# A hybrid decoder step on one core: part-time constants become pages, the keys of the last block are split anew in each pass, and scheduling leads are set per half pass

## The chip, the core and the metric

The kernel runs on one core of one Trainium2 chip. The metric is the device time of one launch in microseconds (us), the median over runs. A profiled execution has a span (first to last instruction) and its own time, which is a little longer. The engines are PE (matrix), PEld (its weight loads), DVE (vector), ACT (scalar), POOL and SP, whose queue issues all DMAs of this kernel. Each engine executes its instructions in the order in which the program lists them.

## What is computed

One inference step of a two-branch layer, for a prompt of 2048 positions and for 8 sample sequences of one position, with width 1024 and float32 data. Cut to what matters:

```python
mod = silu(c) @ w_ada + b_ada                      # shift, scale, gate: 6 groups of 512 columns
h = rms_norm(x, norm_g) * (1 + scale) + shift
u = h @ w_in                                       # 43 column tiles of 128
o_a, wkv_new, shift_new = rwkv_mix(u_shifted, ...) # recurrence with a 64x64 state per head
q, k = rms_norm(q), rms_norm(k)
o_b = sliding_window_attention(q, k, v, window=128, bias, sinks)
merged = sigmoid(g_a) * ((o_a * silu(z_a)) @ w_o_a) + sigmoid(g_b) * ((o_b * silu(z_b)) @ w_o_b)
y = x + gate * (merged @ w_out)
```

The sample group uses the same weights, a stored 64x64 state per head (`state_wkv`), the last projected row and a cache of 128 keys and values.

## The kernel before, in words

**Passes and lines.** The 2048 positions are cut into four passes of 512 (pass 0 to 3). Pass 1 carries the 8 sample columns too, so its dense matmuls come in two pieces of 260 columns. A pass is 59 dense lines: 43 for the projections, in the order of ORDER (decay and rate, then r, k, v of four head pairs, k, v, four q, four z_b, four z_a, eight pairs of gates), 8 for the merge and 8 for the output. A line is 24 matmuls of 128x128 by 512, because each float32 product is made of three products of fp32r halves (`hi`, `lo`). In pass 0 the halves of the weights are made on ACT and DVE and written to DRAM; later passes load them (`weights`, L725).

**Recurrence.** `rwkv(g)` (L1548) does two head pairs: `prep_pair` (L969) makes the products inside chunks of 64; `inverses` (L1059) inverts the triangular matrices by a loop of 31 pairs of DVE instructions (a multiplication and a TENSOR_REDUCE on the tile `nl`), sends the result through DRAM (`d2`), transposes it on DVE (STREAM_TRANSPOSE) and finishes with two sets of 32x32 matmuls on PE; then comes the chain of 8 chunks, each three sets of 64-wide matmuls with copies and additions between them. This text calls the DVE loop with its round trip the solve; there is one per half pass, two per pass. `attention()` (L1553) does the k, v, q and z_b lines and four blocks of 128 queries (`attend`, L1237). With MIDDLE true (L1588) each pass does half 0 of the recurrence, then attention, then half 1.

**Sample work.** In pass 1 `sample_rwkv` (L1306) works through the stored state in four blocks: a load of `swkv` (L1366), some fifteen DVE operations on 128x512, six matmuls against `blocks`, and a store `out_wkvs`. `sample_attention` (L1399) does the cached attention.

**The order of the work.** The program is recorded first and then put in order by `schedule` (L286): an event-driven list scheduler with a cost for each operation, which picks on each engine the ready operation of the lowest priority number. That number is six times the line's index, less a lead. WLEAD (5000) is for weight loads, ELEAD (6000) for what empties a dense line's PSUM tile, and the table LEADS (L109) has one number per kind of step (prep, inv, chain, gn, att, sample and so on) and pass. A lead of thousands exceeds a whole pass (354), so in effect it ranks the kinds of work against each other on each engine. `places` (L321) holds an operation back until a tile is free: CAPS gives 75 pages `p` of 128x520 float32, 8 weight tiles `w`, one `nl`, 3 dense PSUM tiles `d` and 5 others `g`. The engines then run in the order that `schedule` wrote.

**Names that the change touches.** CAPS L108, LEADS L109, ADA L124, MIDDLE L127, `xst` L662, `sct` and `sc32` L688, `ada` L745, `us` L819, `kprev` L820 and L1583, `Lead` L829, `make_h` L860, `keys` L1216, `attend` L1237. ADA says in which order the first four groups of `w_ada` are taken; with False the group is split into fp32r halves (a cast and a subtraction on 128x512 and two matmuls per page), with True it is multiplied as float32 (nine rows, no split). `so` and `sob` are the sample results, `us` the sample columns of all 43 lines.

Of the kernel before, what the change touches and what calls it, by code (L numbers as in the profile page):

```python
# [87 lines left out]
def _constants():  # L88
# [18 lines left out]

CAPS = {"p": 75, "s": 11, "t": 14, "w": 8, "nl": 1, "d": 3, "g": 5}  # L108
LEADS = {  # L109
    "prep": (2490.0, 3436.9, 460.9, 3438.6),  # L110
    "inv": (2996.1, 5954.0, 5871.1, 5871.1),
    "chain": (3475.6, 3475.6, 3475.6, 3475.6),
    "gn": (2855.6, 4741.8, 4539.0, 2629.7),
    "wd": (2207.5, 3240.1, 1705.2, 3248.2),
    "norm": (4852.3, 820.0, 820.0, 820.0),
    "att": (4680.1, 4726.2, 4352.4, 4642.8),
    "sample": (1285.3, 1285.3, 1562.2, 1562.2),
    "bias": (2948.2, 5008.5, 5008.5, 5008.5),
    "h": (3088.9, 3088.9, 3088.9, 3109.5),
    "x": (209.4, 253.7, 253.7, 253.7),  # L120
}
WLEAD, ELEAD = 5000.0, 6000.0
HGATE = 6
ADA = ((2, False), (3, False), (0, True), (1, False))  # L124
EARLY, PLACE = 1, 3
KORDER = True
MIDDLE = True  # L127
FULL = dict(start=True, stop=True)
# [380 lines left out]
def hybrid_step_kernel(ctx: ExitStack, tc: tile.TileContext, A, O):  # L509
# [151 lines left out]
    ct = Sm([128, 8, 9])  # L661
    xst = K([128, 8, NB], "xst")  # L662
    dma(ct, A["ct"])
    dma(vec, A["vec"])
    dma(cst, A["cst"])
    dma(xst, A["xsT"])
    ident, mask = (cst[:, CST[n]:CST[n] + 128] for n in ["ident", "mask"])
# [19 lines left out]
    zero(eps[:, 2:3], KAPPA)  # L687
    sct = K([128, 8, 18], "sct", F32R)  # L688
    sc32 = K([128, 8, 9], "sc32")
    tht = Sm([128, 8, 9])  # L690
# [127 lines left out]
    zero(Sst)  # L818
    us = K([128, len(ORDER), NB], "us")  # L819
    kprev = [K([128, 128], f"kprev{i}", F32R) for i in range(4)]  # L820
    vprev = K([128, 128], "vprev")
# [4 lines left out]

    st = {"mm": [], "q": 0}

    class Lead:  # L829


        def __getitem__(self, name):
            return LEADS[name][min(st["q"], 3)]

# [25 lines left out]
    def make_h(q):  # L860
        sample = q == SQ
        w = W if sample else CH
        xs, acc = [], None
        for k in range(8):
            x = P([128, w])
            with after(*st.get("gate", ())):
                dma(x[:, 0:CH], A["xT"][k, :, q * CH:(q + 1) * CH])
                if sample:
                    copy(x[:, CH:W], xst[:, k, :], "dve/pool")
# [37 lines left out]
    def dense(key, epi):  # L907

        wt = early.pop(key, None) or weights("w_in", INDEX[key])
        for c0, n in st["segs"]:  # L910
            ps = pr.tile("d", [128, n])
            mm3(ps, wt, range(8), st["hk"], c0, n)
            m = min(c0 + n, CH) - c0
            with at(ELEAD):
                epi(ps[:, 0:m], c0, m)
                if c0 + n > CH:
                    copy(us[:, INDEX[key], :], ps[:, m:n])
        step_line()
# [296 lines left out]

    def keys(x):  # L1216

        out = [P([128, CH], F32R) for _ in range(4)]
# [17 lines left out]

    def attend(q, n, qn, kk, vt, bt, zb):  # L1237
        k0 = 128 if (q == 0 and n == 0) else 0
# [66 lines left out]

    def sample_rwkv(lw):  # L1306
        prev = Sm([128, 13, NB])
        dma(prev, A["sshift"])
# [46 lines left out]
        mul(bv, ps, v)  # L1355
        o = K([128, 4, NB], "so")
        idv = Sm([128, 64])
# [40 lines left out]

    def sample_attention():  # L1399
        iq, ik, iv = (INDEX[n, 0] for n in ("q", "kb", "vb"))  # L1400
        qk = Sm([128, 5, NB])
# [69 lines left out]
        add(ob, ob, pb)  # L1471
        o = K([128, 4, NB], "sob")
        obv = ob.rearrange("p (b h) -> p h b", h=8)
# [32 lines left out]
    def finish(q, j, ms, segs):  # L1506
# [5 lines left out]
        for c0, n in segs:  # L1512
# [3 lines left out]
            with at(ELEAD):  # L1516
                stt(xt[:, c0:c0 + m], ps[:, 0:m], modt[:, 16 + j, 0:1], xt[:, c0:c0 + m], ALU.mult, ALU.add)
                if c0 + n > CH:
                    t = Sm([128, NB])
                    mul(t, ps[:, m:n], modt[:, 16 + j, 1:9])  # L1520
                    add(t, t, xst[:, j, :])
                    dma(O["ysT"][:, j, :], t)
# [13 lines left out]
    for q in range(NQ):  # L1536
# [16 lines left out]
        def attention():  # L1553
            if q == 0:
                with at(LEAD["bias"]):
                    bias_table()
            x = plain(("kb", 0))
            with at(LEAD["norm"]):
                normed(x, vc("kg"))
                if q == NQ - 1:  # L1560
                    dma(O["kwp"], x[:, CH - 128:CH])
                kk = keys(x)
            x = plain(("vb", 0))
# [8 lines left out]
            here = line[0] * 6.0  # L1572
            zb = [gate_z(("zb", p)) for p in range(4)]
            pr.key = here - LEAD["att"]
            bt = [[P([128, 2, 256]) for _ in range(2)] for _ in range(2)]
# [146 lines left out]
```

## Time and profile before

| what | value |
|---|---|
| median of 3 runs | 1905.62 us (1904.24 to 1906.92) |
| profiled execution, own time | 1904.95 us |
| its span | 1903.1 us |
| mean granted PE clock | 0.984 |
| instructions in the span | 32620 |
| DMA | 343.20 MB, mean 180 GB/s |

The profiled execution's own time lies 0.67 us below the median of the runs, and its span 1.85 us below its own time. In the timeline a row gives start and length, engine, source line, operation, tiles and count; in square brackets stands how long the engine had been idle and what ended the wait. Almost all vector and scalar operations have line L538 and almost all dense matmuls L579, since helpers record them, so rows are told apart by their tiles and shapes. A float32 matmul counts as two instructions in the profile and as one in the program's order.

### The profile page before, as it was taken

Reading aid. Unit: us, or ns where it says so; the run is one execution under the profiler, and the core shown is the slowest. Engines: PE = TensorE matmul, PEld = TensorE weight load, DVE = VectorE, ACT = ScalarE, POOL = GpSimd, SP = SyncE. Lnnn points to the kernel's source line nnn. Section 1 sums busy time; section 2 is a strip of 40 time slices with the busy share of each in tenths; the row PEclk is TensorE's granted clock in tenths of the full one; section 3 lists DMA queues with packets and bytes.
Section 4 is the critical chain, followed back from the end, with each engine's and each line's share of the span. In section 5 each row is a group of like instructions: output and inputs, shape, how many; then the busy total and the mean of one; then the engine's idle time right before and its main releaser. Section 6 shows DMA issues by size and latency. Waiting matters only on the chain.

```text
span 1903.1 us, 32620 instructions
## 1 busy us (share of the span) xinstructions
PE 1807.5 (95%) x12544; PEld 1444.5 (76%) x12544; DVE 1302.0 (68%) x3138; ACT 798.5 (42%) x1605; POOL 93.9 (5%) x170
## 2 busy tenths in 40 slices
PE   6899999999999799899999999999999999999999
PEld 2667666677799778798998786677788787677787
DVE  8889979459377869792835795964563885894351
ACT  6667545353157355323504544521422562651300
POOL 0000210000000001010000100100000000100000
PEclk9999999999999899999999999999999999999999
DMA  9475537667845413453676453145467454236355
GB/s 335 175 265 213 172 110 273 222 231 283 320 158 175 145 68 102 161 189 118 211 245 201 145 183 119 67 157 186 150 228 249 158 177 141 72 125 194 113 192 187
DMA packets 162456, 343.20 MB, mean 180 GB/s; under 512 B 65485, under 2 KB 69246, under 8 KB 162300
## 3 DMA queue, kind: packets, MB, share of 16 engines
q1 hardware_dynamic: 162300, 341.11, 52.6%
q8 instruction: 99, 1.62, 0.3%
q14 instruction: 57, 0.47, 0.1%
HBM read 263.09 MB, written 77.96 MB: 179 GB/s over the span
## 4 chain that ended last, share of the span: by engine, by line
PE 48%; DVE 18%; ACT 4%; DMA 2%; issue 1%; SPq 1%; DVEq 0%; ACTq 0%
PE d L579 39%; DVE p L538 17%; PE g L597 5%; ACT p L538 3%; PE g L579 2%; PE g L604 2%; ACT L538 1%; DMA p<-in_xT 1%; DMA p<-d 1%; SPq L613 1%; DMA p<-in_swkv 0%; DVE t L538 0%; DMA w<-lo_w_in 0%; DVE s L538 0%; DMA d<-p 0%
## 5 line engine op out<-in xcount | busy, mean ns | idle before, releaser
L579 PE MATMUL d<-p,w 128*128 128x512 f32 (+1 forms) x7080 | 1457.4, 356 | 27.4 <-DVE w L538 15.8
L579 PEld LDWEIGHTS d<-p,w 128*128 128x128 f32 x7080 | 1140.5, 190 | 229.6 <-DVE w L538 26.8
L538 DVE TENSOR_TENSOR p<-p,p 128x512 fp32r<-128x512 f32 (+4 forms) x597 | 358.4, 624 | 33.8 <-ACT p L538 21.8
L597 PE MATMUL g<-p,p 128*64 128x64 f32 (+6 forms) x3952 | 229.1, 245 | 19.4 <-DVE p L538 16.6
L597 PEld LDWEIGHTS g<-p,p 128*64 128x64 f32 (+4 forms) x3952 | 174.7, 144 | 85.8 <-DVE p L538 27.0
L538 ACT COPY p<-g 64x128 f32<-64x128 f32 (+4 forms) x339 | 124.0, 377 | 138.9 <-PE g L597 89.9
L538 ACT CAST p<-p 128x512 fp32r<-128x512 f32 (+2 forms) x201 | 121.5, 621 | 135.6 <-DVE p L538 132.6
L538 ACT ACT_TABLE_LOAD x109 | 139.8, 1283 | 22.9 <-PE g L579 20.4
L538 ACT ACTIVATE p<-d 128x512 f32<-128x512 f32 (+1 forms) x120 | 61.4, 512 | 209.0 <-PE d L579 208.6
L538 DVE TENSOR_TENSOR p<-g,s 64x128 f32<-64x128 f32 (+1 forms) x124 | 40.5, 326 | 141.4 <-PE g L597 136.8
L538 DVE TENSOR_TENSOR p<-p,nl 128x2 f32<-128x2 f32 (+30 forms) x248 | 126.9, 512 | 8.9 <-DMA p<-in_idl 3.7
L538 ACT ACTIVATE p<-d,vec 128x511 f32<-128x511 f32 (+1 forms) x65 | 38.9, 603 | 214.8 <-PE d L579 178.5
L538 DVE SCALAR_TENSOR_TENSOR p<-d,modt,p 128x512 f32<-128x512 f32 (+2 forms) x40 | 25.7, 644 | 124.7 <-PE d L579 115.1
L538 ACT ACTIVATE p<-p 128x512 f32<-128x512 f32 (+2 forms) x161 | 98.1, 633 | 17.4 <-DVE p L538 9.7
L538 DVE TENSOR_TENSOR w<-w,w 128x1024 fp32r<-128x1024 f32 x58 | 70.8, 1221 | 41.2 <-PE d L579 23.5
L579 PE MATMUL g<-p,blocks 128*128 128x512 f32 x202 | 81.8, 436 | 17.5 <-ACT p L538 11.0
L538 ACT CAST w<-w 128x1024 fp32r<-128x1024 f32 x59 | 61.9, 1050 | 83.7 <-PE d L579 51.6
L538 DVE SCALAR_TENSOR_TENSOR p<-p,d 128x512 f32<-128x512 f32 (+1 forms) x120 | 69.3, 579 | 36.9 <-PE d L579 35.8
L538 DVE TENSOR_TENSOR p<-g,cst 64x256 f32<-64x256 f32 (+1 forms) x192 | 88.6, 507 | 3.9 <-PE g L597 3.1
L538 DVE TENSOR_REDUCE p<-p 128x1 f32<-128x2 f32 (+30 forms) x248 | 86.7, 349 | 5.3
L604 PE MATMUL g<-cst,p 128*128 128x128 f32 (+1 forms) x457 | 74.3, 285 | 8.3 <-DVE p L538 7.5
L604 PEld LDWEIGHTS g<-cst,p 128*128 128x128 f32 (+1 forms) x457 | 54.8, 144 | 31.2 <-DVE p L538 12.2
(159 smaller groups left out, 1060.2 us busy)
## 6 DMA issues: line engine op xcount, KB each, us to landing
w<-hi_w_in SPq DMA_DIRECT2D x129, 512.0 KB, 3.6
w<-lo_w_in SPq DMA_DIRECT2D x129, 512.0 KB, 4.5
w<-in_w_in SPq DMA_DIRECT2D x43, 512.0 KB, 4.8
hi_w_in<-w SPq DMA_DIRECT2D x43, 512.0 KB, 3.5
lo_w_in<-w SPq DMA_DIRECT2D x43, 512.0 KB, 4.2
p<-in_xT SPq DMA_DIRECT2D x64, 256.0 KB, 5.8
p<-in_w_ada SPq DMA_DIRECT2D x48, 256.0 KB, 5.5
w<-hi_w_o SPq DMA_DIRECT2D x24, 512.0 KB, 3.6
```

Of the source, the lines that this page charges most:

```text
L538: lambda e: getattr(ENG[e], engs[e])(res(out), *(res(x) for x in a), **{n_: res(v) for n_, v in k.items()}),
L579: pr.rec({"pe": mm_cost(out, lhsT, rhs)}, lambda e: nc.tensor.matmul(res(out), res(lhsT), res(rhs), **k), [out], [lhsT, rhs], table=(part( ...
L597: nc.tensor.matmul(res(out), res(lhsT), res(rhs), **k)
L604: pr.rec({"pe": 2 * _free_size(in_) / 2400.0 + 0.003}, lambda e: nc.tensor.transpose(res(out), res(in_), res(idn)), [out], [in_, idn], tab ...
L613: lambda e: nc.sync.dma_start(out=res(out), in_=res(in_)),
```

## The change

1. `xst`, `us`, `so` and `sob` share one page, which is allocated in pass 1 and filled there (the load of `xst` moves from the start of the program into `make_h`). `sct` and `sc32` become pages that live through pass 0. CAPS gives 77 pages in place of 75.
2. The keys of the last block of a pass are kept once, in float32 (`klast`), and the four fp32r forms are made anew at the start of the next pass by `keys`; before, four fp32r copies were kept (`kprev`).
3. ADA takes the groups 0, 2, 1, 3, two of them split and two whole; before 2, 3, 0, 1 with one whole.
4. LEADS has eight numbers per kind, one for each half of a pass; `attend` sets its priority for each block.
5. MIDDLE is replaced by STAGES: pass 1 does both halves of the recurrence and then attention; the other passes keep attention in the middle.

```diff
-CAPS = {"p": 75, "s": 11, "t": 14, "w": 8, "nl": 1, "d": 3, "g": 5}
+CAPS = {"p": 77, "s": 11, "t": 14, "w": 8, "nl": 1, "d": 3, "g": 5}
 LEADS = {
...
-    "sample": (1285.3, 1285.3, 1562.2, 1562.2),
+    "sample": (5619.9, 5482.5, 7295.5, 7295.5, 7295.5, 7295.5, 7295.5, 5619.9),
...
-ADA = ((2, False), (3, False), (0, True), (1, False))
+ADA = ((0, False), (2, True), (1, False), (3, True))
-MIDDLE = True
+STAGES = ('0A1', '01A', '0A1', '0A1')
...
-    xst = K([128, 8, NB], "xst")
-    dma(xst, A["xsT"])
...
-    sct = K([128, 8, 18], "sct", F32R)
-    sc32 = K([128, 8, 9], "sc32")
+    sct = P([128, 8, 18], F32R)
+    sc32 = P([128, 8, 9])
...
-    us = K([128, len(ORDER), NB], "us")
-    kprev = [K([128, 128], f"kprev{i}", F32R) for i in range(4)]
+    klast = K([128, 128], "klast")
...
-            return LEADS[name][min(st["q"], 3)]
+            return LEADS[name][2 * min(st["q"], 3) + st["half"]]
...
+        if sample:
+            n = len(ORDER)
+            page = P([128, n + 16, NB])
+            st.update({"us": page[:, 0:n], "xst": page[:, n:n + 8], "so": page[:, n + 8:n + 12], "sob": page[:, n + 12:n + 16]})
+            with after(*st.get("gate", ())):
+                dma(st["xst"], A["xsT"])
...
-                kk = keys(x)
+                kprev = []
+                if q > 0:
+                    before = P([128, 4, 128], F32R)
+                    kprev = keys(klast, [before[:, i, :] for i in range(4)])
+                kk = keys(x, [P([128, CH], F32R) for _ in range(4)])
+                copy(klast, x[:, CH - 128:CH], "dve/pool")
...
             for n in range(4):
-                attend(q, n, qn, kk, vt, bt, zb)
-            for i in range(4):
-                copy(kprev[i], kk[i][:, CH - 128:CH], "dve/pool")
+                st["half"] = n // 2
+                pr.key = here * 6.0 - LEAD["att"]
+                attend(q, n, qn, kk, kprev, vt, bt, zb)
...
-        if MIDDLE:
-            rwkv(0)
-            yb = attention()
-            rwkv(1)
-        else:
-            rwkv(0)
-            rwkv(1)
-            yb = attention()
+        for stage in STAGES[min(q, 3)]:
+            if stage == "A":
+                yb = attention()
+            else:
+                rwkv(int(stage))
```

**How the order moves.** On PE, pass 0 keeps its order after the `w_ada` groups. The counts below are of dense matmuls in the order of PE, for before and after: from the start of pass 1 to its first 32x32 matmul 840 and 965; from there to the first 32x32 matmul of the second half 966 and 403; from the first 32x32 matmul to the last product of attention 238 and 814 in pass 1, 141 and 168 in pass 2, 134 and 148 in pass 3. On DVE, 450 rows stand between the transposes of the first half's solve and those of the second in pass 1 before; after, 164 stand there, and 428 from the first half's transposes to the end of attention. In DVE's whole order there are 20 TENSOR_TENSOR fewer (POOL has 20 more) and 26 COPY fewer (ACT has 26 more).

PE in pass 1, at the end of the first half's solve, before (`p_1203` is the transposed solve, rows of 128x260 are dense lines, 128x256 are attention's products of q and k):

```order
L579 MATMUL d_220<-p_925_4603,w_1170_6181 128x260
L579 MATMUL d_220<-p_924_4595,w_1171_6189 128x260
L597 MATMUL g_221<-p_1203_6477,p_1053_5408 32x32 x16
L597 MATMUL g_221<-p_1203_6477,p_1097_5691 32x32 x16
L597 MATMUL g_222<-p_1107_5757,p_1134_5932 128x256
L597 MATMUL g_222<-p_1114_5805,p_1134_5932 128x256
```

The same place after (`p_1228` is the transposed solve):

```order
L579 MATMUL d_211<-p_860_4304,w_1196_6467 128x260
L579 MATMUL d_211<-p_864_4321,w_1196_6467 128x260
L597 MATMUL g_214<-p_1228_6701,p_1042_5374 32x32 x16
L597 MATMUL g_214<-p_1228_6701,p_1080_5666 32x32 x16
L579 MATMUL d_211<-p_860_4304,w_1198_6476 128x260
L579 MATMUL d_211<-p_872_4356,w_1196_6467 128x260
```

Attention is no longer there: eleven dense matmuls stand between the two sets of 32x32 matmuls in place of eight products of attention.

SP's queue in pass 1 around the second load of the stored state, before (`nl` is the solve's tile of the second half, `w` are weight tiles):

```order
L613 DMA d_1_95<-p_1432_7820 32x8x32 x2
L613 DMA out_wkvs<-p_1400_7634 128x512
L613 DMA nl_1467_8028<-d_1_95 64x1024 x2
L613 DMA w_1474_8059<-hi_w_in_158 128x1024
L613 DMA w_1476_8064<-lo_w_in_159 128x1024
L613 DMA p_1477_8069<-in_swkv 128x512
```

The same queue after, around the second and third loads:

```order
L613 DMA out_wkvs<-p_1317_7362 128x512
L613 DMA w_1438_8197<-hi_w_in_159 128x1024
L613 DMA w_1444_8220<-lo_w_in_160 128x1024
L613 DMA p_1446_8232<-in_swkv 128x512
L613 DMA w_1468_8361<-hi_w_in_161 128x1024
L613 DMA w_1469_8368<-lo_w_in_162 128x1024
L613 DMA out_wkvs<-p_1446_8232 128x512
L613 DMA p_1479_8424<-in_swkv 128x512
```

The loads of `nl` no longer stand ahead of the second load; they come before the first one. Now the third load stands directly behind the store of the second block, and the fourth behind that of the third.

More of the change, by code (lines that the diff above doesn't have):

```diff
@@ L106, in _constants @@
     return c, one, np.eye(128, dtype=np.float32)[::-1], idl
-CAPS = {"p": 75, "s": 11, "t": 14, "w": 8, "nl": 1, "d": 3, "g": 5}
+CAPS = {"p": 77, "s": 11, "t": 14, "w": 8, "nl": 1, "d": 3, "g": 5}
 LEADS = {
[L110 to L116, printed above, removed]
-    "sample": (1285.3, 1285.3, 1562.2, 1562.2),
-    "bias": (2948.2, 5008.5, 5008.5, 5008.5),
-    "h": (3088.9, 3088.9, 3088.9, 3109.5),
-    "x": (209.4, 253.7, 253.7, 253.7),
+    "prep": (2430.9, 2430.9, 3436.9, 3436.9, 452.9, 452.9, 3438.6, 3438.6),
+    "inv": (2996.1, 2996.1, 5811.5, 5811.5, 5933.5, 5933.5, 5960.9, 5960.9),
+    "chain": (3475.6, 3475.6, 3475.6, 3463.5, 7297.1, 7297.1, 3457.1, 3475.6),
+    "gn": (2855.6, 3546.9, 4741.8, 195.1, 4539.0, 4539.0, 2629.7, 2629.7),
+    "wd": (2207.5, 2207.5, 3240.1, 3240.1, 1757.7, 1757.7, 3248.2, 3248.2),
+    "norm": (4852.3, 4852.3, 820.0, 820.0, 796.4, 820.0, 820.0, 820.0),
+    "att": (4680.1, 4566.4, 4726.2, 4726.2, 4352.4, 4352.4, 4642.8, 4642.8),
+    "sample": (5619.9, 5482.5, 7295.5, 7295.5, 7295.5, 7295.5, 7295.5, 5619.9),
+    "bias": (2948.2, 2948.2, 5008.5, 5008.5, 5008.5, 3968.7, 5008.5, 5008.5),
+    "h": (3088.9, 3088.9, 3088.9, 3088.9, 3084.9, 3084.9, 2964.3, 3084.9),
+    "x": (390.0, 390.0, 390.0, 394.3, 390.0, 390.0, 0, 390.0),
 }
@@ L825, in hybrid_step_kernel @@
            for i in range(2)]
-    st = {"mm": [], "q": 0}
+    st = {"mm": [], "q": 0, "half": 0}
     class Lead:
         def __getitem__(self, name):
-            return LEADS[name][min(st["q"], 3)]
+            return LEADS[name][2 * min(st["q"], 3) + st["half"]]
     LEAD = Lead()
@@ L868, in make_h @@
                 if sample:
-                    copy(x[:, CH:W], xst[:, k, :], "dve/pool")
+                    copy(x[:, CH:W], st["xst"][:, k, :], "dve/pool")
             sq = P([128, w])
@@ L916, in dense @@
                 if c0 + n > CH:
-                    copy(us[:, INDEX[key], :], ps[:, m:n])
+                    copy(st["us"][:, INDEX[key], :], ps[:, m:n])
         step_line()
@@ L1214, in queries, with keys @@
         return out
-    def keys(x):
-        out = [P([128, CH], F32R) for _ in range(4)]
+    def keys(x, out):
         for e, h in enumerate((lo, hi)):
@@ L1235, in values, with attend @@
         return vt
-    def attend(q, n, qn, kk, vt, bt, zb):
+    def attend(q, n, qn, kk, kprev, vt, bt, zb):
         k0 = 128 if (q == 0 and n == 0) else 0
@@ L1306, in sample_rwkv @@
     def sample_rwkv(lw):
+        us = st["us"]
         prev = Sm([128, 13, NB])
@@ L1355, in sample_rwkv @@
         mul(bv, ps, v)
-        o = K([128, 4, NB], "so")
+        o = st["so"]
         idv = Sm([128, 64])
@@ L1399, in sample_attention @@
     def sample_attention():
+        us = st["us"]
         iq, ik, iv = (INDEX[n, 0] for n in ("q", "kb", "vb"))
@@ L1471, in sample_attention @@
         add(ob, ob, pb)
-        o = K([128, 4, NB], "sob")
+        o = st["sob"]
         obv = ob.rearrange("p (b h) -> p h b", h=8)
@@ L1520, in finish @@
                     mul(t, ps[:, m:n], modt[:, 16 + j, 1:9])
-                    add(t, t, xst[:, j, :])
+                    add(t, t, st["xst"][:, j, :])
                     dma(O["ysT"][:, j, :], t)
@@ L1548, in rwkv @@
         def rwkv(g):
+            st["half"] = g
             for p in (2 * g, 2 * g + 1):
@@ L1553, in attention @@
         def attention():
+            st["half"] = 0
             if q == 0:
@@ L1571, in attention @@
                     qn.append(queries(x))
-            here = line[0] * 6.0
+            here = line[0]
             zb = [gate_z(("zb", p)) for p in range(4)]
-            pr.key = here - LEAD["att"]
+            pr.key = here * 6.0 - LEAD["att"]
             bt = [[P([128, 2, 256]) for _ in range(2)] for _ in range(2)]
@@ L1580, in attention @@
             for n in range(4):
-                attend(q, n, qn, kk, vt, bt, zb)
-            for i in range(4):
-                copy(kprev[i], kk[i][:, CH - 128:CH], "dve/pool")
+                st["half"] = n // 2
+                pr.key = here * 6.0 - LEAD["att"]
+                attend(q, n, qn, kk, kprev, vt, bt, zb)
             copy(vprev, vt[:, 3], "dve/pool")
@@ L1586, in attention @@
             return zb
-        if MIDDLE:
-            rwkv(0)
-            yb = attention()
-            rwkv(1)
-        else:
-            rwkv(0)
-            rwkv(1)
-            yb = attention()
+        for stage in STAGES[min(q, 3)]:
[3 more added lines that the diff above has]
+                rwkv(int(stage))
+        st["half"] = 0
         if sample:
@@ L1599, in hybrid_step_kernel @@
             sob = sample_attention()
-            silu2(sob, us[:, INDEX["zb", 0]:INDEX["zb", 0] + 4, :])
+            silu2(sob, st["us"][:, INDEX["zb", 0]:INDEX["zb", 0] + 4, :])
             for p in range(4):
@@ L1607, in hybrid_step_kernel @@
             if sample:
-                silu2(so, us[:, INDEX["za", 0]:INDEX["za", 0] + 4, :])
+                silu2(so, st["us"][:, INDEX["za", 0]:INDEX["za", 0] + 4, :])
             ya = []
```

## The prediction

> **What bounds the kernel now.** I read the page first, then the busy time by stages, the waits of PE, and the timeline around the two longest of them. The page's first part:
>
> ```profile
> PE 1807.5 (95%) x12544; PEld 1444.5 (76%) x12544; DVE 1302.0 (68%) x3138; ACT 798.5 (42%) x1605; POOL 93.9 (5%) x170
> ```
>
> PE is busy 95% of the span, and the change takes almost no matmul away, so only the 95.6 us in which PE is idle (1903.1 - 1807.5) and the time that it works slowly can be won. The table of stretches shows where the idle time lies: first length, then busy time of PE, PEld, DVE, ACT and POOL, then the granted clock.
>
> ```profile
> 24.00:41.30 17.30, 16.43 (x61) 5.41 (x62) 15.87 (x31) 8.57 (x15) 0.60 (x4) 1.00 1.05 392
> 524.00:658.50 134.50, 123.09 (x1004) 119.09 (x1002) 104.59 (x262) 74.63 (x138) 6.67 (x9) 0.98 0.51 166
> 658.50:745.00 86.50, 81.89 (x884) 67.81 (x885) 64.03 (x219) 50.22 (x146) 9.17 (x18) 0.94 0.19 64
> 745.00:865.50 120.50, 110.97 (x864) 106.94 (x862) 100.39 (x253) 35.48 (x79) 8.67 (x10) 0.96 0.55 178
> 865.50:1012.00 146.50, 146.35 (x1487) 140.43 (x1487) 68.47 (x156) 37.06 (x78) 3.25 (x11) 1.00 0.57 195
> 1012.00:1153.00 141.00, 136.88 (x675) 109.87 (x673) 108.82 (x275) 72.53 (x125) 8.76 (x13) 1.00 0.53 172
> 1153.00:1250.00 97.00, 90.50 (x793) 62.54 (x794) 77.31 (x219) 52.77 (x138) 9.89 (x11) 0.95 0.24 78
> 1597.00:1695.00 98.00, 90.66 (x812) 63.53 (x813) 77.14 (x222) 53.08 (x139) 9.67 (x13) 0.95 0.24 79
> ```
>
> Pass 1 runs from 524 to 1012: PE is idle for 11.4 + 4.6 + 9.5 + 0.2 = 25.7 us in it, nearly all of that before 865, while DVE is nearly full. After 865 PE lacks nothing and DVE is less than half busy. Pass 2's part with chain and attention (1153 to 1250) loses 6.5 us, pass 3's 7.3 us. Where PE idles in pass 1, its waits say:
>
> ```profile
> PE g L597 <- DVE p L538: 12.3, 7, 9.5
> PE g L579 <- ACT p L538: 7.3, 4, 6.7
> ```
>
> Two single waits, 9.5 and 6.7 us, are most of it. A slow clock follows them; these stretches of the same table have a granted clock of 0.50:
>
> ```profile
> 652.00:669.00 17.00, 9.43 (x150) 8.68 (x151) 7.96 (x29) 4.46 (x12) 0.30 (x1) 0.50 0.20 32
> 802.00:808.80 6.80, 4.86 (x18) 4.49 (x19) 4.65 (x11) 1.61 (x3) 0.00 (x0) 0.50 0.31 123
> 1157.00:1163.80 6.80, 6.80 (x78) 4.97 (x80) 2.71 (x8) 1.46 (x5) 0.00 (x0) 0.50 0.01 3
> ```
>
> Work at half clock loses half its time: 9.43 / 2 = 4.7 us and 4.86 / 2 = 2.4 us in pass 1, and up to 6.8 / 2 = 3.4 us in pass 2.
>
> **The first wait: the solve.** PE, DVE and SP around 658 us (the number in brackets is the idle time before the row):
>
> ```profile
> 637.55 11.45 PE L579 MATMUL d<-p,w 128*128 128x260 f32 x94
> 658.50 0.31 PE L597 MATMUL g<-p,p 32*32 32x32 f32 x2 [9.50 <-DVE p L538]
> 651.74 0.69 DVE L538 TENSOR_REDUCE p<-p 128x16 f32<-128x512 f32 x1
> 652.46 1.26 SPq L613 DMA_DIRECT2D d<-p  x2
> 658.01 0.90 DVE L538 STREAM_TRANSPOSE p<-p 32x256 f32<-32x256 f32 x2 [4.93 <-DMA p<-d]
> ```
>
> The loop ends on DVE at 652.4, the round trip through DRAM takes until 658, and PE had run out of its 94 dense matmuls at 649. These take 11.45 / 94 = 0.12 us each. From pass start to this place the order of PE has 840 dense matmuls before and 965 after: 125 x 0.12 = 15 us more cover. But two more pairs of preparation stand on DVE ahead of the solve now. In the row 524.00:658.50 DVE has 134.5 - 104.6 = 29.9 us free. A pair's preparation takes a share of the 100.39 us that DVE works from 745 to 865, where two pairs, sample work and the second loop (some 25 us) lie; I take 15 us for a pair at most, 30 us for two. So DVE needs up to 30 us more, fits it into 29.9 + 15 us, and the wait shrinks. I take 8 of the 9.5 us as won; the bounds are 9.5 and nothing.
>
> **The second wait: a load of the stored state.** SP, DVE and PE:
>
> ```profile
> 793.41 1.13 SPq L613 DMA_DIRECT2D nl<-d  x2
> 795.69 0.42 SPq L613 DMA_DIRECT2D p<-in_swkv  x1
> 802.54 0.69 DVE L538 TENSOR_TENSOR p<-p,s 128x512 f32<-128x512 f32 x1 [2.69 <-DMA p<-in_swkv]
> 803.94 0.80 PE L579 MATMUL g<-p,blocks 128*128 128x512 f32 x1 [6.72 <-ACT p L538]
> 812.19 0.38 SPq L613 DMA_DIRECT2D p<-in_swkv  x1
> 820.14 0.69 DVE L538 TENSOR_TENSOR p<-p,s 128x512 f32<-128x512 f32 x1
> ```
>
> The load is queued behind two loads of `nl`, which wait for the solve's data, and it is used 802.54 - 795.69 = 6.9 us after its issue; PE stands 6.72 us. The third load has 820.14 - 812.19 = 8.0 us until its use and costs nothing. After, `nl` is loaded long before, so this wait goes: -6.7 us. But the third and fourth loads stand right behind the stores of the block before, which wait for DVE, and DVE's order has about 15 rows between the store's last addition and the next use. At 100.39 / 253 = 0.40 us a row that is 6 us against the 6.9 us of this load: a wait of about 1 us on DVE at one or two loads. Sum -5 us; from -6.7 (no new wait) to +7 (two new waits as long as the old, 2 x 6.7 - 6.7).
>
> **The half clock in pass 1.** If both waits go, 4.7 + 2.4 = 7.1 us of slow work go with them. A short slow stretch stays, as in pass 2 (1157.00:1163.80), where no wait is longer than 2 us. I take -6 us, from -7.1 to 0. The Trainium skill ("TensorE: Matmul & The Clock Gate", the part on the clock gate and its table of two states) says that the array drops to half its clock after an idle window of about 3.4 us and recovers after about as long of sustained work. The rows at 652 and 802 agree with that; the row at 1157 does not, since PE is busy through all of it. By that rule alone pass 2 and 3 could win nothing from their half clock, and the sum below would be 2 us less.
>
> **What takes their place in pass 1.** The work of 658 to 865 is not removed, only arranged anew: chain 0 now runs beside the second solve, chain 1 beside the sample work and the start of attention. From the first transposes to the end of attention the order of DVE has 428 rows after; 450 stood between the two solves' transposes before, and these took 64.03 + 100.39 = 164.4 us of DVE. So DVE has 428 x 164.4 / 450 = 156 us there. PE has 814 dense matmuls in that stretch, 98 us, against 966 before, 116 us; before, PE was busy 81.89 + 110.97 = 192.9 us there. Less 18 us of dense work, and with one chain more and two preparations fewer, that is some 175 us. PE stays the longer of the two, but closely, and every chain step, sample block and attention block waits on a DVE that is 156 / 175 = 89% full. Before, the same stretch lost 4.6 + 9.5 - 6.7 = 7.4 us to waits that are not the load. I add 4 us: +4, from 0 to +15 (twice the 7.4 again).
>
> **Passes 2 and 3.** Their waits behind the solve are short:
>
> ```profile
> 1147.82 4.79 PE L579 MATMUL d<-p,w 128*128 128x512 f32 x20
> 1156.89 0.75 PE L579 MATMUL d<-p,w 128*128 128x512 f32 x1 [1.82 <-DVE p L538]
> 1159.42 4.21 PE L579 MATMUL d<-p,w 128*128 128x512 f32 x9
> ```
>
> A dense matmul takes 4.79 / 20 = 0.24 us, at half clock 4.21 / 9 = 0.47. From the solve to the end of attention the order has 27 dense matmuls more in pass 2 (141 to 168) and 14 more in pass 3 (134 to 148): 6.5 and 3.4 us of cover, against 6.5 and 7.3 us of idle time. Six dense matmuls now stand between the two sets of 32x32 ones where one stood, which covers the 1.82 us wait nearly (5 x 0.24 = 1.2 us). Not all cover falls where a wait is; I take half, 3 and 2 us, together -5, from -11 (all 9.9 us and 1 us of clock) to +3, since chain and attention are mixed anew.
>
> **The start.** Before the first dense matmul two groups of `w_ada` are split in place of three:
>
> ```profile
> 14.03 0.61 PE L579 MATMUL d<-p,sct 128*18 128x512 f32 x1 [14.03 <-ACT p L538]
> 32.13 3.60 PE L579 MATMUL d<-p,sc 128*9 128x512 f32 x8
> 34.93 3.26 DVE L538 TENSOR_TENSOR p<-p,p 128x512 fp32r<-128x512 f32 x5
> 33.66 1.66 ACT L538 CAST p<-p 128x512 fp32r<-128x512 f32 x3
> 38.79 2.71 PE L579 MATMUL d<-p,sct 128*18 128x512 f32 x11
> 41.34 0.62 PE L579 MATMUL d<-p,w 128*128 128x512 f32 x2
> ```
>
> A group fewer takes 8 x 3.26 / 5 = 5.2 us from DVE and 8 x 1.66 / 3 = 4.4 us from ACT. PE gives up 16 matmuls of 2.71 / 11 = 0.25 us, 3.9 us, and gets a whole group, 2 x 3.60 = 7.2 us: 3.3 us more. PE is busy 16.43 of 17.30 us from 24 to 41.3 (it starts at 14.03, as before), so the 3.3 us count; DVE is busy 15.87 of 17.30 us, so its 5.2 us count where PE waits for it afterwards. The two nearly cancel: 0, from -4 to +3.
>
> **The rest.** The page for the sample columns, the constants as pages, and two more pages add no instruction on PE. The new split of the last keys is 8 small operations per pass on half the partitions, in three passes, less 4 copies in each:
>
> ```profile
> L538 ACT COPY p<-g 64x128 f32<-64x128 f32 (+4 forms) x339 | 124.0, 377 | 138.9 <-PE g L597 89.9
> ```
>
> At 377 ns that is 24 x 0.377 = 9 us, shared by ACT (42% busy) and DVE, ahead of attention, whose first products have dense lines before them. That cover hides it: 0; without it 3 us per pass.
>
> **The sum.** Pass 1: -8 - 5 - 6 + 4 = -15. Passes 2 and 3: -5. Start and rest: 0. From the profiled execution's 1904.95 us (span 1903.1 and 1.85 around it; 0.67 us below the median) that gives 1885 us.
>
> **Rivals.** *All idle time of pass 1 goes.* 25.7 us of waits and 7.1 us of clock, with 10 us in passes 2 and 3: 1904.95 - 42.8 = 1862 us. For it speaks that the second half of pass 1 has room (68.47 of 146.5 us on DVE); against it, that DVE stays 89% full in the crowded stretch.
>
> *The waits move and nothing is won.* The solve ends as late as before because its loop shares DVE with four preparations, and DVE has 20 other rows between the end of the loop and the transposes where 2 stood (8 us at 0.40). Then only the load's wait and its clock go (6.7 + 2.4), and the crowded stretch gives back 7.4: about 1903 us. The same comes out if the tables and pages change little of what is waited for.
>
> *Slower: the sample's chain starves PE.* The sample lead (1285 to 7295) now lies above what empties the dense tiles (6000), and each of four blocks runs load, DVE, PE, DVE, store, load, with the next load behind the store. If DVE's 15 rows between store and use take less than the load's 6.9 us, in-order DVE stands still, epilogues behind it keep the three dense PSUM tiles, and PE stops: three loads at 6.7 us and their clock at 2.4 are 27 us. Less the old load (9.1) and the solve (8): 1904.95 + 10 = 1915 us. It decides at about 6 us of DVE work per block; I counted 6, so it is close, but DVE also has attention to do meanwhile.
>
> **How the numbers follow.** Forecast 0.59, all idle time 0.12, nothing won 0.14, slower 0.15. The forecast's own terms end at 1872 and 1899 when two of them are at a bound. The range, 1864 to 1909 us, takes in the case without gain and half of the best one, and part of the slower one. About 0.2%, 3.8 us, is what a measurement of this kernel can tell from no change. Faster by more: 0.59 + 0.12 + a third of the case without gain, 0.76; within it 0.10; slower by more 0.14.
>
> **What would show it.** Right: in pass 1 no wait of PE over 3 us before the first 32x32 matmul nor at a `blocks` matmul of the sample, pass 1 about 15 us shorter than 488 us, no half clock of 17 us; passes 2 and 3 each 2 to 3 us shorter; first dense matmul at 41 to 44 us. Wrong: a wait of DVE on `in_swkv` or on the round trip of `d` with PE idle behind it, idle time of PE in pass 1 above 20 us, or a pass 0 that changes by more than 4 us.

## The result and the profile after

The changed kernel takes 1883.12 us (median of 4 runs, 1882.18 to 1886.82); the kernel before, run beside it, 1904.93 us (1902.86 to 1906.92). The ratio is 0.9889 (95% interval 0.9872 to 0.9907), about 21 us less; all ratios below, too, are to the kernel before, run beside the kernel in question. Of all runs in this text one was slow, a run of the changed kernel with 75 pages that took 2895 us at a granted clock of 0.57, and it is left out of the figures. The profiled execution has a span of 1880.9 us. The forecast was 1885 us, and the whole came out so. Its parts did not, and the rest of this text is about them.

The page's first part of the changed kernel:

```profile
PE 1797.0 (96%) x12544; PEld 1438.7 (76%) x12544; DVE 1284.6 (68%) x3098; ACT 803.7 (43%) x1629; POOL 110.5 (6%) x184
```

PE's idle time is 1880.9 - 1797.0 = 83.9 us where it was 95.6, so idle time explains 12 us of the 22; the other 10 are matmuls that ran at a faster clock or stalled less. The same stretches by pass show where. The borders are the first dense matmuls of the passes; first the kernel before, then the changed one, with length, busy time of PE, PEld, DVE, ACT and POOL, granted clock, DMA share and GB/s:

```profile
41.34:524.24 482.90, 454.62 (x2771) 335.14 (x2770) 368.76 (x808) 245.57 (x445) 25.05 (x38) 0.99 0.64 227
524.24:1011.71 487.47, 461.77 (x4232) 433.82 (x4231) 337.39 (x886) 197.38 (x441) 27.76 (x48) 0.97 0.48 160
1011.71:1456.63 444.92, 433.56 (x2731) 333.55 (x2729) 287.20 (x698) 172.46 (x352) 23.83 (x38) 0.99 0.50 164
1456.63:1903.10 446.47, 431.72 (x2727) 332.91 (x2725) 275.42 (x674) 158.03 (x328) 15.53 (x28) 0.99 0.46 153
```

```profile
42.59:523.14 480.55, 453.21 (x2763) 334.37 (x2763) 367.04 (x805) 244.53 (x446) 24.22 (x37) 0.99 0.64 227
523.14:1009.69 486.55, 462.83 (x4232) 433.48 (x4230) 332.20 (x871) 198.85 (x452) 38.77 (x57) 0.97 0.48 160
1009.69:1444.27 434.58, 425.91 (x2730) 330.05 (x2729) 283.42 (x692) 177.02 (x363) 24.05 (x40) 1.00 0.51 168
1444.27:1880.90 436.63, 426.41 (x2727) 330.73 (x2725) 269.91 (x661) 160.33 (x334) 21.52 (x32) 0.99 0.47 157
```

Pass 1, from which 15 us were forecast, gives 0.9. Passes 2 and 3, from which 5 were forecast, give 10.3 and 9.8. The start costs 1.2 us, and pass 0 gives 2.4, which is too little to read anything from: single executions of this same pass 0, in the kernels below, take from 477.2 to 480.6 us.

**Pass 1.** The two waits of before, 9.5 us at 658 and 6.72 us at 804, are gone, and DVE waits for no load of the stored state. But the longest wait of PE behind DVE is now 12.3 us. The waits of PE (total, number, longest) and the timeline around 767 us (PE, DVE, SP):

```profile
PE g L597 <- DVE p L538: 14.4, 7, 12.3
```

```profile
746.47 8.98 PE L579 MATMUL d<-p,w 128*128 128x260 f32 x73
767.72 0.31 PE L597 MATMUL g<-p,p 32*32 32x32 f32 x2 [12.27 <-DVE p L538]
...
744.59 0.69 DVE L538 TENSOR_REDUCE p<-p 128x16 f32<-128x512 f32 x1
...
767.23 1.83 DVE L538 STREAM_TRANSPOSE p<-p 32x256 f32<-32x256 f32 x4 [16.85 <-DMA p<-d]
...
733.94 5.78 SPq L613 DMA_DIRECT2D out_kws<-p  x1
...
745.31 4.56 SPq L613 DMA_DIRECT2D d<-p  x2
749.97 3.27 SPq L613 DMA_DIRECT2D w<-lo_w_in  x1
753.34 0.27 SPq L613 DMA_DIRECT2D out_vws<-p  x1
755.03 12.32 SPq L613 DMA_DIRECT2D p<-d  x8
```

This is the second solve: its loop ends on DVE at 745.3, and its transposes start at 767.2. The round trip through DRAM took 22 us, where that of 652 to 658 took 5.5. The eight loads that bring the solve back needed 12.32 us to be issued. Ahead of them stands `out_vws`, a store of the sample's value cache with 127 rows. What the DMA engines moved meanwhile (a window of 2 us):

```profile
DMA packets 25, 0.05 MB, mean 26 GB/s; under 512 B 0, under 2 KB 0, under 8 KB 25
...
q1 hardware_dynamic: 25, 0.05, 6.6%
```

Twenty-five packets in 2 us, one behind the other at 0.08 us, and 6.6% of sixteen engines, which is about the share of one: one engine works, fifteen stand. The trace has 127 such packets of 2 KB in a row, from 756.5 to 766.7 us, so the 127 rows take 127 x 0.08 = 10.2 us. Behind the wait PE runs slowly for 20.5 us:

```profile
759.80:780.30 20.50, 11.95 (x172) 11.04 (x173) 3.77 (x10) 3.87 (x10) 0.00 (x0) 0.50 0.29 83
```

The stage in which the forecast had the new waits, from the first solve's transposes over 428 rows of DVE to the end of attention, takes 209.7 us:

```profile
672.70:882.40 209.70, 193.31 (x2020) 170.01 (x2019) 147.77 (x428) 95.91 (x245) 15.92 (x27) 0.94 0.39 125
```

**Passes 2 and 3.** Around the 32x32 matmuls of the first half in pass 2, before and then after:

```profile
1154.39 0.69 PE L597 MATMUL g<-p,p 32*32 32x32 f32 x30 [0.22 <-DVE p L538]
...
1157.57 1.92 PE L597 MATMUL g<-p,p 32*32 32x32 f32 x64
```

```profile
1153.03 1.20 PE L597 MATMUL g<-p,p 32*32 32x32 f32 x64
1154.16 1.66 PE L579 MATMUL d<-p,w 128*128 128x512 f32 x6
1155.75 1.20 PE L597 MATMUL g<-p,p 32*32 32x32 f32 x64
```

The second set takes 1.92 us before and 1.20 after. The stretches that were at half clock (two of 3.4 and two of 6.8 us in the two passes before) are down to one of 3.4 us. The windows of before in pass 2 and those of after at the same place:

```profile
1153.00:1157.00 4.00, 1.74 (x65) 1.40 (x65) 3.09 (x8) 1.86 (x5) 0.00 (x0) 1.00 0.80 269
1157.00:1163.80 6.80, 6.80 (x78) 4.97 (x80) 2.71 (x8) 1.46 (x5) 0.00 (x0) 0.50 0.01 3
...
1228.60:1232.00 3.40, 3.40 (x13) 2.84 (x13) 3.37 (x10) 3.05 (x10) 0.00 (x0) 0.51 0.00 0
```

```profile
1153.00:1157.00 4.00, 4.00 (x136) 3.35 (x135) 2.38 (x5) 2.06 (x6) 0.00 (x0) 1.00 0.23 91
1157.00:1163.80 6.80, 6.80 (x68) 4.71 (x68) 2.55 (x9) 2.15 (x8) 0.40 (x1) 1.00 0.47 158
```

The slow stretch follows four microseconds in which PE was busy for 1.74; at the same place after, with PE busy throughout, it does not come. That is not the whole of it. The changed kernel has a stretch of 3.4 us at half clock in pass 1 with no idle time of PE in the 3.41 us ahead of it, only matmuls of 8 and of 64 columns (two rows of the timeline, then the 3.4 us ahead of the slow stretch and the stretch itself):

```profile
820.92 1.85 PE L579 MATMUL g<-s,p 128*128 128x8 f32 x16
822.70 3.35 PE L597 MATMUL g<-p,p 128*64 128x64 f32 x32
...
821.27:824.68 3.41, 3.41 (x41) 3.25 (x40) 1.48 (x4) 0.80 (x2) 0.00 (x0) 1.00 0.53 206
824.70:828.10 3.40, 3.40 (x14) 3.01 (x13) 3.25 (x8) 1.05 (x2) 0.00 (x0) 0.50 0.00 0
```

So the busy time of PE alone does not say whether the clock halves.

### The profile page after: what moved, and what is told of

It reads as the page before. It is cut to its first block, busy times and chain, and to the rows that moved or that the text cites. A ratio compares the mean times of both kernels' runs of the same rounds, so it can differ in the third digit from the quotient of the medians.

```text
span 1880.9 us, 32643 instructions
## 1 busy us (share of the span) xinstructions
PE 1797.0 (96%) x12544; PEld 1438.7 (76%) x12544; DVE 1284.6 (68%) x3098; ACT 803.7 (43%) x1629; POOL 110.5 (6%) x184
## 4 chain that ended last, share of the span: by engine, by line
PE 54%; DVE 14%; ACT 3%; DMA 2%; issue 1%; POOL 0%; SPq 0%; DVEq 0%; ACTq 0%
PE d L579 44%; DVE p L538 13%; PE g L597 6%; PE g L579 2%; ACT p L538 2%; PE g L604 2%; ACT L538 1%; DMA p<-d 1%; DMA p<-in_xT 1%; DMA d<-p 0%; DVE s L538 0%; POOL p L538 0%; DMA w<-lo_w_in 0%; SPq L613 0%; DMA w<-hi_w_in 0%
## 5 line engine op out<-in xcount | busy, mean ns | idle before, releaser
L538 DVE TENSOR_TENSOR p<-p,p 128x512 fp32r<-128x512 f32 (+6 forms) x573 | 348.7, 632 | 50.6 <-ACT p L538 42.9
L597 PE MATMUL g<-p,p 128*64 128x64 f32 (+5 forms) x4000 | 227.0, 243 | 15.5 <-DVE p L538 14.4
L538 ACT COPY p<-g 64x128 f32<-64x128 f32 (+4 forms) x365 | 131.3, 370 | 141.1 <-PE g L597 74.4
L538 ACT CAST p<-p 128x512 fp32r<-128x512 f32 (+2 forms) x189 | 113.9, 618 | 126.7 <-DVE p L538 118.7
L538 DVE TENSOR_TENSOR p<-p,nl 128x2 f32<-128x2 f32 (+30 forms) x248 | 127.2, 513 | 13.8 <-DMA p<-in_idl 8.8
L538 ACT ACTIVATE p<-p 128x512 f32<-128x512 f32 (+2 forms) x161 | 98.6, 632 | 23.7 <-DVE p L538 15.9
L538 DVE TENSOR_REDUCE p<-p 128x1 f32<-128x2 f32 (+31 forms) x252 | 89.0, 353 | 4.9
L538 POOL TENSOR_TENSOR p<-p,p 64x256 f32<-64x256 f32 (+2 forms) x52 | 60.1, 1172 | 508.7 <-DVE p L538 257.3
```

What stands on the lines that cost most here:

```text
L538: lambda e: getattr(ENG[e], engs[e])(res(out), *(res(x) for x in a), **{n_: res(v) for n_, v in k.items()}),
L597: nc.tensor.matmul(res(out), res(lhsT), res(rhs), **k)
```

## The experiments

For orientation, one profiled execution of each kernel: the passes' lengths from first dense matmul to first dense matmul (pass 3: to its last), and the dense matmuls between the two sets of 32x32 matmuls in the first half of passes 2 and 3. All are read from the timeline of PE.

| kernel | pass 0 | pass 1 | pass 2 | pass 3 | between the sets |
|---|---|---|---|---|---|
| before | 482.9 | 487.5 | 444.9 | 441.9 | 1, 1 |
| changed | 480.6 | 486.5 | 434.6 | 432.1 | 6, 6 |
| changed, stores split | 477.2 | 473.7 | 434.4 | 432.8 | 6, 6 |
| before, stores split | 480.0 | 480.8 | 444.3 | 442.2 | 1, 1 |
| changed, stores split, old pass 1 | 479.8 | 477.8 | 434.7 | 431.6 | 6, 6 |
| changed, old leads in passes 2, 3 | 478.1 | 488.0 | 438.7 | 430.6 | 9, 9 |
| before, new leads in passes 2, 3 | 482.9 | 487.6 | 444.5 | 436.5 | 1, 0 |
| pages only | 482.0 | 494.5 | 439.6 | 429.8 | 9, 9 |
| before, 76 pages | 482.5 | 487.7 | 444.1 | 438.8 | 1, 1 |
| changed, 75 pages | 514.6 | 544.7 | 449.1 | 436.1 | 1, 0 |
| before, keys kept once | 555.9 | 482.3 | 453.9 | 440.1 | 1, 1 |

### The two stores of 127 rows

The edit, in the helper that issues all DMAs, leaves the order of all engines as it was:

```diff
+    def send(out, in_):
+        if out.shape[0] == 127:
+            nc.sync.dma_start(out=out[0:112], in_=in_[0:112])
+            nc.sync.dma_start(out=out[112:127], in_=in_[112:127])
+        else:
+            nc.sync.dma_start(out=out, in_=in_)
...
-                   lambda e: nc.sync.dma_start(out=res(out), in_=res(in_)),
+                   lambda e: send(res(out), res(in_)),
```

In the changed kernel:

> The changed kernel, with each of the two stores of 127 rows of the sample's value cache issued as 112 and 15 rows; the order of the work is the same. Theory: a store of 127 rows goes through one DMA engine, 127 packets of 2048 bytes at 0.084 us each, 10.7 us, and the second solve's round trip stood behind it; so the wait of 12.3 us before the 32x32 matmuls at 767 goes, with most of the 20.5 us at half clock behind it: -16 us (-22 to -10), 1867 us. Rival: the round trip is slow by its own packets of 128 bytes and by the weight loads on SP's queue: no change, 1883 us.

Measured: 1866.41 us, ratio to before 0.9802 (0.9781 to 0.9823). The timeline of SP and PE at the same place:

```profile
745.97 0.38 SPq L609 DMA_DIRECT2D out_vws<-p  x1
746.41 0.43 SPq L610 DMA_DIRECT2D out_vws<-p  x1
747.58 4.82 SPq L612 DMA_DIRECT2D p<-d  x8
...
752.66 1.00 PE L597 MATMUL g<-p,p 32*32 32x32 f32 x34
```

The eight loads are issued in 4.82 us in place of 12.32, PE does not wait, and pass 1 falls from 486.5 to 473.7 us. The theory holds, with its size; this kernel is faster than the changed one and the one before. In the kernel before:

> The kernel before, with the same split of the two stores. Theory: there the stores stand between 762 and 785 us, where PE hardly waits, and the wait of 6.7 us at 804 comes from the two loads of the solve ahead of the stored state's load: within 3 us of before, 1905 us. Rival: the blocked DMA engine delays the sample work as a whole and the 6.7 us go with it: 1896 us or less.

Measured: 1896.68 us, ratio 0.9969 (0.9952 to 0.9985). Here the rival was right. The wait of 6.72 us at 804 is gone, as the waits of PE behind ACT in the kernel before and in this one show (total, number, longest):

```profile
PE g L579 <- ACT p L538: 11.6, 11, 6.7
```

```profile
PE g L579 <- ACT p L538: 4.8, 9, 1.1
```

In the kernel before the chain is to be seen on SP:

```profile
762.13 4.97 SPq L613 DMA_DIRECT2D out_vws<-p  x2
767.20 9.86 SPq L613 DMA_DIRECT2D out_kws<-p  x1
777.11 3.00 SPq L613 DMA_DIRECT2D d<-p  x2
```

The issue of `out_kws` stands for 9.86 us behind two stores of 127 rows, then the solve's data leave late, then `nl` (793.41) and the stored state (795.69) are loaded late. With the split these two are issued at 784.0 and 788.0. The forecast had stopped at the last link, the two loads of `nl`.

### What the new order of pass 1 is worth

The changed kernel with split stores, with `STAGES` and pass 1's leads as before:

```diff
-STAGES = ('0A1', '01A', '0A1', '0A1')
+STAGES = ('0A1', '0A1', '0A1', '0A1')
...
-    "inv": (2996.1, 2996.1, 5811.5, 5811.5, 5933.5, 5933.5, 5960.9, 5960.9),
+    "inv": (2996.1, 2996.1, 5954.0, 5954.0, 5933.5, 5933.5, 5960.9, 5960.9),
```

> The changed kernel with the split stores, and pass 1 with attention in the middle and the leads that pass 1 had before. Theory: the new order of pass 1 is worth what the forecast said once the stores no longer block it: pass 1 takes 481 us as in the kernel before with split stores, in place of 474, so 1873 us, while passes 2 and 3 keep their 434 and 433 us. Rival one: the new order is worth nothing and pass 1 stays at 474, 1866 us. Rival two: passes 2 and 3 owe their gain to what the new pass 1 hands on, and go back to 444 and 442 us: 1892 us.

Measured: 1872.96 us, ratio 0.9841 (0.9826 to 0.9856). The time is the one that the theory gave, in part by luck: pass 1 takes 477.8 us, between the two values expected, and 2.6 us of the difference lie in pass 0 (479.8 against 477.2 us). So the new order is worth some 4 us in pass 1, at most the 7 us of the whole, once the stores let it, and passes 2 and 3 owe it nothing.

### Leads or pages in passes 2 and 3

The changed kernel with the old leads in the last four of each eight, for instance

```diff
-    "chain": (3475.6, 3475.6, 3475.6, 3463.5, 7297.1, 7297.1, 3457.1, 3475.6),
+    "chain": (3475.6, 3475.6, 3475.6, 3463.5, 3475.6, 3475.6, 3475.6, 3475.6),
```

> The changed kernel with the leads of passes 2 and 3 of the kernel before. Theory: those leads alone bring the 20 us that passes 2 and 3 won: 1903 us, and half clock again behind the first 32x32 matmuls of both passes. Rival: the two pages and the new copies of the keys bring it: 1883 us. Half of each would be 1893 us.

Measured: 1883.67 us, ratio 0.9896 (0.9875 to 0.9918): the theory fell. The two passes take 869.3 us, 2.6 more than in the changed kernel and 17.5 less than before. The kernel before with the new leads in passes 2 and 3:

```diff
-    "chain": (3475.6, 3475.6, 3475.6, 3475.6),
+    "chain": (3475.6, 3475.6, 7297.1, 3457.1),
```

> The kernel before with the changed kernel's leads in passes 2 and 3, one number per pass (that of the first half), and nothing else. Theory: 20 us less, 1885 us, with no half clock behind the first 32x32 matmuls of passes 2 and 3. Rival: without the two pages the leads bring nothing: 1905 us.

Measured: 1899.26 us, ratio 0.9971 (0.9958 to 0.9984), a quarter of what was expected; pass 2 does not move. Next the pages, first taken away:

```diff
-CAPS = {"p": 77, "s": 11, "t": 14, "w": 8, "nl": 1, "d": 3, "g": 5}
+CAPS = {"p": 75, "s": 11, "t": 14, "w": 8, "nl": 1, "d": 3, "g": 5}
```

> The changed kernel with 75 pages in place of 77, all else as it is. Theory, since the leads of passes 2 and 3 have been shown to bring only 3 us: the two pages bring the gain of passes 2 and 3, which go back to some 443 and 441 us, with half clock behind the first 32x32 matmuls: 1900 us. Rival: the keys kept once bring it: 1883 us.

Measured: 1992.90 us, ratio 1.0468 (1.0439 to 1.0497). The direction is right and the size is not: passes 2 and 3 lose 14.5 and 4 us, but passes 0 and 1 lose 92 (dense lines of one mix with the other's there). One wait of PE in it:

```profile
838.15 0.31 PE L597 MATMUL g<-p,p 32*32 32x32 f32 x2 [57.84 <-DVE p L538]
```

Then the keys alone, in the kernel before with its 75 pages:

```diff
-    kprev = [K([128, 128], f"kprev{i}", F32R) for i in range(4)]
+    klast = K([128, 128], "klast")
...
-                kk = keys(x)
+                kprev = []
+                if q > 0:
+                    before = P([128, 4, 128], F32R)
+                    kprev = keys(klast, [before[:, i, :] for i in range(4)])
+                kk = keys(x, [P([128, CH], F32R) for _ in range(4)])
+                copy(klast, x[:, CH - 128:CH], "dve/pool")
```

> The kernel before with the keys of the last block kept once and split anew, and nothing else. Theory (pages): no gain, 1904 us, or up to 5 us slower, since the split takes one page for a time. Rival: passes 2 and 3 win 9 us each as in the changed kernel: 1886 us.

Measured: 1981.16 us, ratio 1.0413 (1.0396 to 1.0429). Far outside both; the largest wait stands in pass 0:

```profile
388.80 0.31 PE L597 MATMUL g<-p,p 32*32 32x32 f32 x2 [48.61 <-DVE p L538]
```

The keys won nothing, as the theory said, but that they cost 79 us at 75 pages nobody had priced: pass 0 splits no kept keys, so what it loses must come from the order that the planner then writes. Then the pages together with the new keys and nothing else, which is the changed kernel with all old leads, the old `ADA` and attention in the middle:

```diff
-ADA = ((0, False), (2, True), (1, False), (3, True))
-STAGES = ('0A1', '01A', '0A1', '0A1')
+ADA = ((2, False), (3, False), (0, True), (1, False))
+STAGES = ('0A1', '0A1', '0A1', '0A1')
```

> The changed kernel with all the old numbers and orders: leads, order of the w_ada groups and attention in the middle of pass 1 as before. What is left of the change is the pages with a life, the keys kept once and 77 pages. Theory: the pages alone bring the gain of passes 2 and 3 (434 and 432 us in place of 445 and 442), pass 1 stays at 487 us: 1885 us. Rival: pages and leads are needed together, since each alone was shown to bring little or nothing: 1900 us or more.

Measured: 1889.63 us, ratio 0.9927 (0.9904 to 0.9949). Passes 2 and 3 take 869.4 us together, 17.4 less than before: what is left of the change, pages and keys together, brings seven eighths of the gain there. Pass 1 takes 494.5 us, not 487. By the timeline a store of 127 rows now holds up the preparation of the second solve (behind it DVE stands 13.2 us for the load of `nl`); a split of the stores was not tried here:

```profile
768.10 2.55 SPq L613 DMA_DIRECT2D out_vws<-p  x1
770.70 6.85 SPq L613 DMA_DIRECT2D d<-p  x2
...
796.69 0.37 PE L604 MATMUL g<-cst,p 64*128 64x64 f32 x1 [11.90 <-DVE p L538]
```

Last, one page more in the kernel before, with its four copies of the keys:

```diff
-CAPS = {"p": 75, "s": 11, "t": 14, "w": 8, "nl": 1, "d": 3, "g": 5}
+CAPS = {"p": 76, "s": 11, "t": 14, "w": 8, "nl": 1, "d": 3, "g": 5}
...
+            page = P([128, n + 16, NB])
```

> The kernel before with its part-time constants as pages and 76 pages in place of 75; the four copies of the keys stay constants. In passes 2 and 3 it has one page more than before, and needs none more. Theory: one page brings part of what the changed kernel won there, 3 to 15 of the 20 us: 1895 us (1889 to 1901). Rival: one page brings nothing: 1903 us.

Measured: 1902.57 us, ratio 0.9998 (0.9984 to 1.0012). The profiled execution shows 3.9 us less in passes 2 and 3, which the times do not confirm. One page more changes nothing; two more, together with the keys kept once, change 17 us. Two more pages with the old four copies of the keys were not run, so the share of each is open. The last column of the table goes with it: at most 1 dense matmul between the sets with 75 or 76 pages, 6 to 9 with 77.

### Why the clock halves

Idle products of the identity among the 32x32 matmuls, in the kernel before, first half of passes 2 and 3. What they write is overwritten or never read.

```diff
+            for i, (out, lhsT, rhs, k) in enumerate(calls):
+                for _ in range(fill * (i in (0, 16))):
+                    nc.tensor.matmul(res(spare), res(ident), res(ident), **FULL)
```

> The kernel before, with six idle 128x128x128 products of the identity (two lots of three, overwritten afterwards) put among the first set of 32x32 matmuls of the first half of passes 2 and 3; they add work that is not needed, some 6 x 0.23 = 1.4 us of PE per place. Theory: the stretches of 6.8 us at half clock at 1157 and 1601 follow because PE streams for less than a third of the 3.41 us before them; with the products it does not, the stretches go and give back 3.4 us each: 6.8 - 2.8 = 4 us faster, about 1900 us. Rival: the clock falls for another reason (the wait of 1.8 us, or the small tiles as such): the stretches stay and the kernel is 2 to 3 us slower, 1906 us.

Measured: 1905.94 us, ratio 1.0011 (1.0000 to 1.0023): no gain, and about 2 us slower as the rival said, though the interval reaches down to no change. The wait of 1.83 us stayed, and so did the slow stretch:

```profile
1157.90:1162.50 4.60, 2.65 (x72) 2.22 (x71) 3.13 (x8) 1.95 (x5) 0.00 (x0) 1.00 0.73 235
1162.50:1169.30 6.80, 6.80 (x84) 5.09 (x84) 2.60 (x8) 1.37 (x4) 0.00 (x0) 0.50 0.01 2
```

PE is still idle for 2 of the 4.6 us ahead of it, and busy for 1.58 of the last 3.41 us, where it was 1.37 before (40%, not less than a third). So the experiment did not make the condition that it was to test. A second one put products behind the first set and ahead of the second too:

```diff
+            {16: (3, ps[:, 1, 4:8, :]), 32: (4, ps[0:32, 0, 0:4, :])} if group in (4, 6) else {})
...
+            {0: (3, ps[:, 1, 4:8, :])} if group in (4, 6) else {})
```

> The kernel before with ten idle products of the identity (128 or 32 by 128, 128 columns) at the first half of passes 2 and 3: three among the first set of 32x32 matmuls, four behind it, three ahead of the second set, so that they lie in the wait of 1.8 us too, where the earlier six did not. Some 10 x 0.23 = 2.3 us of PE per place, of which up to 1.8 lie in the wait. Theory: with PE streaming all through, the stretches of 6.8 us at half clock behind these places go, 3.4 us each: 6.8 - 2 x 1 = about 5 us faster, 1898 us. Rival: the small tiles as such bring the clock down: stretches unchanged, 1 to 4 us slower than before, 1905 us.

Measured: 1904.72 us, ratio 1.0013 (0.9999 to 1.0027): no gain. In pass 2 the slow stretch is gone, in pass 3 it is longer:

```profile
1153.40:1158.50 5.10, 3.40 (x78) 2.81 (x78) 2.90 (x8) 1.95 (x5) 0.00 (x0) 1.00 0.62 215
1158.50:1162.00 3.50, 3.42 (x76) 3.04 (x77) 1.69 (x6) 0.90 (x3) 0.00 (x0) 1.00 0.00 0
1595.40:1598.00 2.60, 2.38 (x71) 2.06 (x72) 1.25 (x3) 0.00 (x0) 0.00 (x0) 1.00 0.73 213
1598.10:1608.30 10.20, 8.64 (x87) 6.95 (x86) 4.49 (x12) 3.28 (x9) 0.00 (x0) 0.50 0.13 50
```

So half clock can follow 2.6 us in which PE is busy for 2.38, most of it small tiles (a wait of 1.60 us stands ahead of them). Over 3.41 us PE is busy for 2.52 ahead of the slow stretch in pass 3, and for 2.63 at the same place in pass 2, where none follows. What brings the clock down is not settled: in most places an emptier window goes ahead of a slow one, but at 824.7 in the changed kernel a full one does. Neither the theory nor the rival (small tiles as such) is shown; in the changed kernel two full sets of 32x32 matmuls pass at 1153 to 1157 without a drop.

## Why the forecast came out, and where it was wrong

The total, 1885 against 1883, is right by luck: two errors of about 15 us cancel, a gain in pass 1 that did not come and one in passes 2 and 3 that was not foreseen.

| term | forecast | measured |
|---|---|---|
| pass 1: wait for the solve | -8 | -9.5 |
| pass 1: load of the stored state | -5 | -6.7 |
| pass 1: half clock | -6 | 0 (27.3 us at half clock before and after) |
| pass 1: new waits | +4 (0 to +15) | +12.3 for one wait, some 3 more to make up the sum |
| passes 2 and 3 | -5 (-11 to +3) | -20.1 |
| start | 0 (-4 to +3) | +1.2 |

- **Pass 1, first two terms.** The mechanism was right for the solve: more dense matmuls stand ahead, and the wait is gone. For the stored state the price was right and the cause only half: the loads of `nl` were late because of the stores of 127 rows (shown by the split in the kernel before).
- **Pass 1, new waits.** This is the step that failed: "PE stays the longer of the two, but closely, and every chain step, sample block and attention block waits on a DVE that is 156 / 175 = 89% full". DVE was not that full. In its 428 rows from the first transposes on it works 147.8 us, nearly as counted, but that is 70% of the 209.7 us of the stage, and PE works 193 us there where 175 were counted. What came was one DMA wait of 12.3 us, and with it the half clock that the forecast had counted as won. The text named the signs to look for, a wait of DVE on the round trip of `d` with PE idle behind it and more than 20 us of idle PE in pass 1 (it is 23.7), and both came; but it had no price for the wait: it counted what stands in SP's queue, and not on how many DMA engines a store runs. With the stores split pass 1 takes 473.7 us, 13.8 less than before and near the 15 of the forecast; but 6.7 of these the split alone gives in the kernel before (480.8 us), so even without this wait the new order is worth half of the 15 or less.
- **Passes 2 and 3.** "The page for the sample columns, the constants as pages, and two more pages add no instruction on PE", and so were set to 0. That they add none is right, that they are worth 0 is the second step that failed: with the pages, the keys kept once and 77 pages, and all leads and orders as before, the planner writes another order, worth 17.4 us in these two passes. The term of -5 counted the idle time alone; idle time gave 2.7 and 4.5 us (444.92 - 433.56 = 11.4 to 8.7, 446.47 - 431.72 = 14.8 to 10.2). The half clock gave up to 5.1 us in pass 2 (10.2 us at half before, none after) and up to 3.4 in pass 3. The remaining 4 us are busy time that was not traced singly.
- **The half clock at 1157.** "the row at 1157 does not, since PE is busy through all of it" looked at the slow stretch. The time ahead of it has to be looked at, and PE was busy for 1.74 of the four microseconds there. The Trainium skill ("TensorE: Matmul & The Clock Gate", the part on the clock gate) lets the clock fall after an idle window of about 3.4 us, in windows that run freely; the slow stretches here last 3.4, 6.8 and 20.5 us, one, two and six such windows, which agrees. That the window has to be idle does not agree: PE was busy for 1.37 of the 3.41 us ahead of 1157, and for all of those ahead of 824.7 in the changed kernel.
- **The stores.** The Trainium skill ("DMA: Bandwidth & Descriptors", the section on why a DMA increments its semaphore by 16) says that a DMA uses the largest number of engines up to 16 that divides the slowest dimension of both its access patterns, and that 127 partitions go to one. The trace agrees (6.6% of sixteen engines, 25 packets in 2 us), and so does the split into 112 and 15 rows. The forecast had not weighed it.
- **Rivals.** The sample's chain did not starve PE: nothing waits for a load of the stored state. "The waits move and nothing is won" is what pass 1 did, by another wait than the one it named. "All idle time of pass 1 goes" did not come, though the split kernel comes near its 1862 us by way of passes 2 and 3.

Open: which held-back operation makes the order of 75 and 76 pages so different from that of 77; how the gain of passes 2 and 3 divides between the two pages and the new keys; what brings the clock down; the new order of the `w_ada` groups, which was not tried alone.

## What to carry to other kernels

Before a gain is put down to an order of work, list the DMAs that stand near its critical round trips, and look at how their rows divide among the DMA engines: a store of 127 rows kept one engine busy for 10 us and held up everything behind it, and cutting both such stores in two gave 17 us. Where a planner hands out buffers, a change in their number can change the whole order (the changed kernel with 75 pages in place of 77 takes 110 us more), and has to be priced like one. A forecast that is right in total should still be taken apart by stage.

## What was not expected of the hardware

- One small DMA can delay unrelated ones: the solve's eight loads of 32 KB took 12.32 us to be issued behind 127 packets of 2 KB, and 4.82 us without. The queue's issue itself stood, 5.78 us (changed kernel) and 9.86 us (before) for one store of 256 KB, which took 0.40 us in both with the stores split.
- A wait of under 2 us among 32x32 matmuls (1.82 us at 1157) stood ahead of 6.8 us at half clock, and matmuls of 8 and 64 columns without any wait ahead of 3.4 us (824.7, changed kernel).
